# A depthwise convolution on four engines: four taps of the even places move to TensorE as float32 diagonal matmuls

## The chip, the cores and the metric

The kernel runs on one core of one Trainium2 chip. A core has TensorE (PE, with its weight loads shown as PEld), VectorE (DVE), ScalarE (ACT), GpSimd (POOL) and SyncE (SP, which issues most DMAs); each engine works through its own instructions in a fixed order and waits for others by semaphores. The metric is the device time of one execution in microseconds (us), lower is better.

## The reference

A decoder trunk with two layers on 1024 tokens of width 1024: a Conformer convolution layer, then a stick-breaking attention layer, each followed by a convolution-gated FFN with a per-layer embedding (PLE). Everything is float32. The part that matters here is the convolution module of the first layer, and the PLE product that needs nothing but the input p:

```python
def causal_dwconv(x, w, b):              # w: 31 taps x 1024 channels, one filter for each channel
    k = w.shape[0]
    y = lax.conv_general_dilated(
        x, w[:, None, :].astype(x.dtype), window_strides=(1,), padding=[(k - 1, 0)],
        dimension_numbers=("NWC", "WIO", "NWC"), feature_group_count=x.shape[-1])
    return y + b

def conformer_conv(x, pw1_w, pw1_b, dw_w, dw_b, ln_g, ln_b, pw2_w, pw2_b):
    h = x @ pw1_w + pw1_b                # 1024 -> 2048
    a, g = jnp.split(h, 2, axis=-1)
    h = a * jax.nn.sigmoid(g)
    h = causal_dwconv(h, dw_w, dw_b)
    h = layer_norm(h, ln_g, ln_b)
    h = jax.nn.silu(h)
    return h @ pw2_w + pw2_b
...
        ple = jax.nn.sigmoid(x @ ple_w_gate[i]) * (p[i] @ ple_w_proj[i])
```

## The kernel before

Products of matrices keep float32 accuracy by splitting each operand into a rounded high part and the rest (type float32r) and adding three matmuls (`mm3`, lines 136 to 139: high by high, high by low, low by high). Such a matmul with 512 columns is one instruction.

The stretch that the change touches is the first 311 us, phase 1 of the first layer. It goes over eight channel tiles c of 128 channels (`KT`, loop from line 528).

- **pw1(c)**, lines 466 to 481: for each half of 512 tokens, 48 matmuls into one of two PSUM tiles `big0` and `big1` (line 470); ACT takes the sigmoid of the gate part (`sg`, line 474), DVE multiplies and writes `hb` (line 476), even tokens in `hb[:, 0]`, odd tokens in `hb[:, 1]`.
- **depthwise(c)**, lines 483 to 522: the 31 taps by a fast two-phase scheme. With even and odd tokens apart, three filters are enough: even taps on even tokens (16 multiply-adds into PSUM `e`, lines 500 and 502), odd taps on odd tokens (15 into PSUM `o`, lines 507 and 509), and the summed taps on the sum of both (16 into `pb` in SBUF). DVE does the first two, one tap in an instruction of 128x512. The third is shared: ACT multiplies (`pr`, line 490), POOL adds (line 491). DVE then joins the three (lines 514, 516 and 520). `e` and `o` are PSUM banks 0 and 1.
- **weights**: for each channel tile two slabs come by DMA, ACT rounds them (line 132) and POOL makes the rest (line 86).
- **the fill**, `ple_proj` (lines 195 to 232): the PLE products of both layers, which depend on nothing before, in eight halves. A half transposes p twice (line 211, into PSUM), ACT and DVE split it into `pTh` and `pTl` (line 215 and line 86), then 24 matmuls for four output tiles, which ACT copies out (line 225) to DRAM. Transposes and products take PSUM banks 2 and 3 in turns (`sm_bank`).
- **after it**: `conv_ln` transposes the result of all channels back by tokens (line 545, into `big0` and `big1` in turns), takes the layer norm (DVE lines 169 to 180 and 547, ACT line 550), `conv_act` transposes again (line 559), takes SiLU (ACT line 562), rounds (line 565) and splits (DVE), and `pw2` multiplies (into PSUM banks). All this is done for the first 512 tokens, then for the others.

The order of the instructions on each engine isn't the order of the code: a scheduler with a model of the times lays out all of them when the kernel is built, by when it thinks that operands are ready. An engine then follows that order, whatever the real times are.

Of the kernel before, what the change touches and what calls it, by code (L numbers as in the profile page):

```python
# [8 lines left out]
F32 = mybir.dt.float32  # L9
# [4 lines left out]
ALU = mybir.AluOpType  # L14
PSUM = bass.MemoryType.PSUM
DRAM = bass.MemoryType.DRAM

P = 128
# [3 lines left out]
HALF = 512  # L22
# [9 lines left out]
NEG = -1.0e30  # L32
HP = 8
N_B = 16
AW = (5 + 6 + 7 + 8) * P
NA = 2
AHEAD = 1
# [14 lines left out]
def trunk_kernel(ctx: ExitStack, tc, x, p, a_pw1_w, a_pw1_b, a_dw_w, a_dw_b, a_ln_g, a_ln_b, a_pw2_w, a_pw2_b,  # L52
                 b_wq, kv_wk, kv_wv, b_wo, ln_mix_g, ln_mix_b, ffn_w_up, ffn_w_gate, ffn_conv_w, ffn_conv_b,
                 ffn_w_down, ple_w_gate, ple_w_proj, ln_ffn_g, ln_ffn_b, out, stop=None):
    nc = tc.nc
# [3 lines left out]
    def pool(name, bufs=1, stack=ctx, **kw):  # L59
        return stack.enter_context(tc.tile_pool(name=name, bufs=bufs, reuse_waits="tile", **kw))  # L60
# [10 lines left out]
    big0 = psum.tile([P, 1024], F32, name="big0")  # L71
    banks = [psum.tile([P, HALF], F32, name=f"bank{i}") for i in range(4)]

    def turns(tiles):
        tiles = list(tiles)

        def nxt():
            tiles.append(tiles.pop(0))
            return tiles[-1]

        return nxt

    bank, acc_bank, sm_bank = (turns(t) for t in (banks, banks[0:2], banks[2:4]))

    def sub_l(eng, l, full, h):
        eng.tensor_tensor(out=l, in0=full, in1=h.bitcast(F32), op=ALU.subtract)  # L86
# [7 lines left out]
    ident, vec_a, vec_b, zero = (ctile[:, a:b] for a, b in ((0, P), (P, 2 * P), (2 * P, 2 * P + 88), (350, 351)))  # L94
# [97 lines left out]
        nc.vector.scalar_tensor_tensor(out=dst, in0=dst, scalar=rstd, in1=b, op0=ALU.mult, op1=ALU.add)  # L192


    def ple_proj(i, sb, dst):

        pT, ws = [], []

# [211 lines left out]
    pp1 = dram.tile([S, D], F32, name="pp1")  # L410

    with ExitStack() as l0:
        big = turns((big0, pool("ps0", 1, l0, space=PSUM).tile([P, 1024], F32, name="big1")))
        res = []
        x1T = [None, None]
        with ExitStack() as ph:
# [5 lines left out]
            def pw1_w(c):  # L422
                return [load_w(w_slab(a_pw1_w[0], slice(0, KT), slice(o + c * P, o + (c + 1) * P)), (KT, P))
                        for o in (D, 0)]
# [54 lines left out]
                                                   op0=ALU.add, op1=ALU.mult)  # L479
                return hb  # L480

            def depthwise(c, hb):
                nc.vector.tensor_tensor(out=hb[:, 2, :], in0=hb[:, 0, :], in1=hb[:, 1, :], op=ALU.add)

                pb = sb.tile([P, HALF], F32, name="pb", bufs=2)
# [2 lines left out]
                for k in range(1, N_B):  # L488
                    pr = sb.tile([P, HALF], F32, name="pr", bufs=3)
                    nc.scalar.mul(pr, hb[:, 2, k:k + HALF], dws[:, c, k:k + 1])  # L490
                    nc.gpsimd.tensor_tensor(out=pb, in0=pb, in1=pr, op=ALU.add)  # L491
                e = acc_bank()
                o = acc_bank()
                os_ = sb.tile([P, 1 + HALF], F32, name="os", bufs=2)
                nc.gpsimd.memset(os_[:, 0:1], 0.0)
                ov = os_[:, 1:]
                for k in range(16):
                    v, w = hb[:, 0, k:k + HALF], dwc[:, c, 2 * k:2 * k + 1]
                    if k == 0:
                        nc.vector.tensor_scalar(out=e, in0=v, scalar1=w, scalar2=None, op0=ALU.mult)  # L500
                    else:
                        nc.vector.scalar_tensor_tensor(out=e, in0=v, scalar=w, in1=e, op0=ALU.mult, op1=ALU.add)  # L502
                    if k == 15:
                        break
                    v, w = hb[:, 1, k + 1:k + 1 + HALF], dwc[:, c, 2 * k + 1:2 * k + 2]
                    if k == 0:
                        nc.vector.tensor_scalar(out=o, in0=v, scalar1=w, scalar2=None, op0=ALU.mult)
                    else:
                        nc.vector.scalar_tensor_tensor(out=ov if k == 14 else o, in0=v, scalar=w, in1=o, op0=ALU.mult,  # L509
                                                       op1=ALU.add)  # L510
# [11 lines left out]

            ys = []
            rowp = Rows()
            fill = ple_proj(0, sb, pp0) + ple_proj(1, sb, pp1)
            w1 = pw1_w(1)
            hb = pw1(0, w0)
            for c in range(KT):
                w0, w1 = w1, pw1_w(c + 2) if c < KT - 2 else None
                nxt = pw1(c + 1, w0) if c < KT - 1 else None  # L530
                ys.append(depthwise(c, hb))
                hb = nxt
            for piece in fill:
                piece()
# [358 lines left out]
```

## Time and profile before

| | us |
|---|---|
| median of 3 runs (2700.6 to 2705.1) | 2701.26 |
| profiled execution, its own time | 2710.24 |
| its span, first to last instruction | 2708.1 |

| busy in the profiled execution | PE | DVE | ACT | POOL |
|---|---|---|---|---|
| whole span, us (share) | 2530.3 (93%) | 1797.4 (66%) | 1045.1 (39%) | 1219.6 (45%) |

Busy time of PE is modelled from overlapping instructions; for PE the distance from one start to the next is the better measure. A row of the timeline gives start, duration, engine, line of the code, output and input by name, count, and in brackets how long the engine had been idle and what it had waited for. A row of the groups by line gives the count, the sum and the mean duration (in ns), then the idle time before.

### The profile page before, as it was taken

Reading aid. Unit: us, or ns where it says so; the run is one execution under the profiler, and the core shown is the slowest. Engines: PE = TensorE matmul, PEld = TensorE weight load, DVE = VectorE, ACT = ScalarE, POOL = GpSimd, SP = SyncE. Lnnn points to the kernel's source line nnn. Section 1 sums busy time; section 2 is a strip of 40 time slices with the busy share of each in tenths; the row PEclk is TensorE's granted clock in tenths of the full one; section 3 lists DMA queues with packets and bytes.
Section 4 is the critical chain, followed back from the end, with each engine's and each line's share of the span. In section 5 each row is a group of like instructions: output and inputs, shape, how many; then the busy total and the mean of one; then the engine's idle time right before and its main releaser. Section 6 shows DMA issues by size and latency. Waiting matters only on the chain.

```text
span 2708.1 us, 34235 instructions
## 1 busy us (share of the span) xinstructions
PE 2530.3 (93%) x13300; PEld 2151.5 (79%) x13300; DVE 1797.4 (66%) x2785; ACT 1045.1 (39%) x1621; POOL 1219.6 (45%) x825
## 2 busy tenths in 40 slices
PE   8996898999999999999999999789899999999995
PEld 6884888987878787878888887589798787787874
DVE  4999769465565655675667677777845555655558
ACT  4556532333223332314555566632333232323231
POOL 3998236534333443413443433544744343333354
PEclk9998999999999999999999999899899999999998
DMA  4114421211111111123111101322111121111121
GB/s 151 47 47 148 163 71 63 86 47 50 47 60 47 55 55 55 40 80 108 46 43 36 55 25 47 129 84 87 63 63 62 48 63 47 47 47 47 47 78 62
DMA packets 149085, 179.12 MB, mean 66 GB/s; under 512 B 6508, under 2 KB 125756, under 8 KB 148924
## 3 DMA queue, kind: packets, MB, share of 16 engines
q1 hardware_dynamic: 144316, 168.56, 19.6%
q10 hardware_dynamic: 4608, 8.39, 0.8%
q8 instruction: 104, 1.70, 0.3%
q14 instruction: 57, 0.47, 0.1%
HBM read 151.76 MB, written 20.97 MB: 64 GB/s over the span
## 4 chain that ended last, share of the span: by engine, by line
PE 68%; DVE 18%; POOL 5%; DMA 3%; issue 3%; ACT 3%; SPq 0%; POOLq 0%; ACTq 0%; DVEq 0%
PE bank L137 13%; PE bank L138 13%; PE bank L139 13%; PE big L137 8%; PE big L139 7%; PE big L138 7%; POOL w L86 3%; PE big L739 2%; POOL pb L491 2%; DVE bank L502 2%; DVE bank L509 2%; DMA w<-in_ffn_w_up 2%; DVE pt L282 2%; PE bank L773 1%; PE more L779 1%
## 5 line engine op out<-in xcount | busy, mean ns | idle before, releaser
L86 POOL TENSOR_TENSOR w<-w 128x512 fp32r<-128x512 f32 (+1 forms) x444 | 757.7, 1720 | 1081.5 <-ACT w L299 697.0
L137 PE MATMUL bank<-w,xT 128*128 128x256 f32 x1280 | 369.7, 291 | 37.7 <-ACT sg L258 23.7
L299 ACT CAST w<-w 128x512 fp32r<-128x512 f32 x308 | 180.1, 619 | 540.2 <-PE bank L139 142.1
L138 PE MATMUL bank<-w,xT 128*128 128x256 f32 x1280 | 368.8, 290 | 2.1 <-POOL w L86 2.1
L139 PE MATMUL bank<-w,xT 128*128 128x256 f32 x1280 | 367.7, 290 | 0.7 <-DVE xT L86 0.6
L137 PEld LDWEIGHTS bank<-w,xT 128*128 128x128 f32 x1280 | 250.8, 197 | 41.0 <-ACT sg L258 25.1
L760 POOL TENSOR_TENSOR res<-res,rr 128x639 f32<-128x639 f32 (+3 forms) x96 | 152.6, 1590 | 259.7 <-DVE rr L758 237.9
L758 DVE TENSOR_TENSOR_SCAN rr<-rr,ctile 128x127 f32<-128x127 f32 (+7 forms) x128 | 195.7, 1550 | 102.5 <-ACT rr L756 102.1
L138 PEld LDWEIGHTS bank<-w,xT 128*128 128x128 f32 x1280 | 251.5, 197 | 3.4 <-POOL w L86 3.0
L139 PEld LDWEIGHTS bank<-w,xT 128*128 128x128 f32 x1280 | 250.2, 196 | 1.7 <-DVE xT L86 1.3
L132 ACT CAST w<-w 128x1024 fp32r<-128x1024 f32 x136 | 142.9, 1051 | 227.5 <-PE bank L138 60.5
L137 PE MATMUL big<-xT,w 128*128 128x512 f32 x544 | 212.3, 390 | 0.4 <-DVE xT L86 0.4
L138 PE MATMUL big<-xT,w 128*128 128x512 f32 x544 | 211.9, 389 | 0.0
L139 PE MATMUL big<-xT,w 128*128 128x512 f32 x544 | 211.9, 389 | 0.0
L294 DVE TENSOR_TENSOR w<-w 128x512 f32<-128x512 f32 x176 | 130.1, 759 | 106.1 <-DMA w<-in_ffn_w_up 52.1
L137 PE MATMUL bank<-xT,w 128*128 128x512 f32 x496 | 200.0, 403 | 0.3 <-DVE m L86 0.2
L138 PE MATMUL bank<-xT,w 128*128 128x512 f32 x496 | 198.2, 400 | 0.0
L139 PE MATMUL bank<-xT,w 128*128 128x512 f32 x496 | 197.8, 399 | 0.0
L383 DVE TENSOR_TENSOR m<-m,bank 128x512 f32<-128x512 f32 x192 | 128.8, 682 | 82.2 <-PE bank L139 82.1
L137 PE MATMUL bank<-w,f 128*128 128x512 f32 x448 | 170.3, 395 | 7.8 <-ACT f L366 4.3
L138 PE MATMUL bank<-w,f 128*128 128x512 f32 x448 | 176.1, 393 | 0.0
L139 PE MATMUL bank<-w,f 128*128 128x512 f32 x448 | 173.8, 391 | 0.0
(162 smaller groups left out, 5941.3 us busy)
## 6 DMA issues: line engine op xcount, KB each, us to landing
w<-in_ffn_w_gate SPq DMA_DIRECT2D x44, 512.0 KB
w<-in_ffn_w_up SPq DMA_DIRECT2D x44, 512.0 KB
w<-in_ffn_w_down SPq DMA_DIRECT2D x44, 512.0 KB
w<-in_a_pw_w SPq DMA_DIRECT2D x32, 512.0 KB
pp<-o ACTq DMA_DIRECT2D x32, 256.0 KB
w<-in_ple_w_gate SPq DMA_DIRECT2D x16, 512.0 KB
w<-pp SPq DMA_DIRECT2D x16, 512.0 KB
w<-in_b_wo SPq DMA_DIRECT2D x16, 512.0 KB
```

The lines of the kernel that those rows point to most:

```text
L86: eng.tensor_tensor(out=l, in0=full, in1=h.bitcast(F32), op=ALU.subtract)
L132: nc.scalar.copy(out=h[:, 0:n], in_=raw)
L137: nc.tensor.matmul(out=o, lhsT=sh, rhs=mh, start=first, stop=False)
L138: nc.tensor.matmul(out=o, lhsT=sh, rhs=ml, start=False, stop=False)
L139: nc.tensor.matmul(out=o, lhsT=sl, rhs=mh, start=False, stop=last)
L282: nc.vector.tensor_tensor(out=f, in0=a, in1=c, op=ALU.subtract)
L294: nc.vector.tensor_tensor(out=out, in0=a, in1=c, op=op)
L299: nc.scalar.copy(out=h, in_=full)
L383: nc.vector.tensor_tensor(out=rv, in0=rv, in1=ps, op=ALU.add)
L491: nc.gpsimd.tensor_tensor(out=pb, in0=pb, in1=pr, op=ALU.add)
L758: nc.vector.tensor_tensor_scan(out=rv[:, i, 1:n][:, ::-1], data0=rv[:, i, 1:n][:, ::-1], data1=zero.broadcast_to([P, n - 1]), initial=1.0, ...
L760: nc.gpsimd.tensor_tensor(out=av[:, :, 0:n - 1], in0=av[:, :, 0:n - 1], in1=rv[:, :, 1:n], op=ALU.mult)
```

## The change

For each channel tile the first four of the sixteen taps on the even tokens leave DVE. ACT writes four diagonal matrices of 128x128 (`dg`, identity times the tap's weight of each channel), and TensorE multiplies them with the shifted `hb`, four plain float32 matmuls of 512 columns that add up in the PSUM bank `e`. DVE adds the other twelve taps onto `e` as before. The matmuls stand in the code ahead of pw1(c+1).

PSUM is dealt out anew: `e` takes banks 0 and 1 in turns over the channel tiles, `o` is always bank 2, and the fill now takes bank 3 and the first halves of `big0` and `big1` in turns.

```diff
@@ -80,7 +81,7 @@
-    bank, acc_bank, sm_bank = (turns(t) for t in (banks, banks[0:2], banks[2:4]))
+    bank, acc_bank = (turns(t) for t in (banks, banks[0:2]))
@@ -410,7 +411,9 @@
-        big = turns((big0, pool("ps0", 1, l0, space=PSUM).tile([P, 1024], F32, name="big1")))
+        big1 = pool("ps0", 1, l0, space=PSUM).tile([P, 1024], F32, name="big1")
+        big = turns((big0, big1))
+        sm_bank = turns((banks[3], big0[:, 0:HALF], big1[:, 0:HALF]))
@@ -479,7 +482,17 @@
-            def depthwise(c, hb):
+            def first_taps(c, hb):
+
+                e = acc_bank()
+                dg = sb.tile([P, N_PE, P], F32, name="dg", bufs=2)
+                for k in range(N_PE):
+                    nc.scalar.mul(dg[:, k], ident, dwc[:, c, 2 * k:2 * k + 1])
+                for k in range(N_PE):
+                    nc.tensor.matmul(out=e, lhsT=dg[:, k], rhs=hb[:, 0, k:k + HALF], start=(k == 0), stop=(k == N_PE - 1))
+                return e
+
+            def depthwise(c, hb, e):
@@ -489,16 +502,13 @@
-                e = acc_bank()
-                o = acc_bank()
+                o = banks[2]
...
-                    if k == 0:
-                        nc.vector.tensor_scalar(out=e, in0=v, scalar1=w, scalar2=None, op0=ALU.mult)
-                    else:
+                    if k >= N_PE:
                         nc.vector.scalar_tensor_tensor(out=e, in0=v, scalar=w, in1=e, op0=ALU.mult, op1=ALU.add)
@@ -522,13 +532,14 @@
             for c in range(KT):
                 w0, w1 = w1, pw1_w(c + 2) if c < KT - 2 else None
+                e = first_taps(c, hb)
                 nxt = pw1(c + 1, w0) if c < KT - 1 else None
-                ys.append(depthwise(c, hb))
+                ys.append(depthwise(c, hb, e))
                 hb = nxt
```

The scheduler lays out the first 320 us anew; from the first columns of pw2 on, the instructions stand on all engines as before. A line of the new code stands 1 to 11 below the same line of the old (line 211 is now 212, line 137 is 138, line 545 is 556, line 559 is 570); the new matmul is line 492.

On PE at the end of pw1(7): `big` and `bank` are PSUM, `praw` the input p, `pTh` and `pTl` its halves. Before, the fill follows, and what is ready of the first token tiles is transposed at once (line 545, five channel tiles of eight):

```order
L139 MATMUL big_100<-xT,w 128x512
L211 MATMUL bank_85<-ctile,praw 128x128 x4
L137 MATMUL bank_84<-w,pTh 128x512
L138 MATMUL bank_84<-w,pTh 128x512
L139 MATMUL bank_84<-w,pTl 128x512
...
L545 MATMUL big_81<-ctile,res 128x128 x5
```

Now, the four taps of the last channel tile (line 492) stand between the fill's first instructions:

```order
L140 MATMUL big_100<-xT,w 128x512
L212 MATMUL big_81<-ctile,praw 128x128 x4
L138 MATMUL bank_85<-w,pTh 128x512
L139 MATMUL bank_85<-w,pTh 128x512
L492 MATMUL bank_83<-hb,dg 128x512 x4
L212 MATMUL big_100<-ctile,praw 128x128 x4
L140 MATMUL bank_85<-w,pTl 128x512
```

For each of the seven channel tiles before, the four stand after the first 27 matmuls of the next tile's pw1. No transposes of line 545 stand near here any more.

On PE around the layer norm: before, the last transposes of line 545 for the first four token tiles stand among the last two halves of the fill, and those of line 559 too (the last half's):

```order
L211 MATMUL bank_84<-ctile,praw 128x128 x4
...
L211 MATMUL bank_85<-ctile,praw 128x128 x4
L559 MATMUL bank_82<-ctile,m 128x128
L559 MATMUL bank_83<-ctile,m 128x128
L545 MATMUL big_81<-ctile,res 128x128 x8
L559 MATMUL bank_82<-ctile,m 128x128
L559 MATMUL bank_83<-ctile,m 128x128
L545 MATMUL big_100<-ctile,res 128x128 x8
L137 MATMUL bank_84<-w,pTh 128x512
```

Now, the first transposes of line 556 (the old 545) stand ahead of the last 12 matmuls of the whole fill, and all others behind them:

```order
L212 MATMUL big_100<-ctile,praw 128x128 x4
L556 MATMUL big_81<-ctile,res 128x128 x8
L138 MATMUL bank_85<-w,pTh 128x512
L139 MATMUL bank_85<-w,pTh 128x512
L138 MATMUL big_100<-w,pTh 128x512
...
L140 MATMUL bank_85<-w,pTl 128x512
L556 MATMUL big_100<-ctile,res 128x128 x8
L556 MATMUL big_81<-ctile,res 128x128 x8
L570 MATMUL bank_82<-ctile,m 128x128
L570 MATMUL bank_83<-ctile,m 128x128
L556 MATMUL big_100<-ctile,res 128x128 x8
```

The layer norm of the first four token tiles has moved from among the fill to its end.

## Rows read from the trace of the kernel before

**Rows 1.** Busy time by stretch: length, engines (instructions), granted clock, DMA share, GB/s
```profile
28.90:204.10 175.20, 175.20 (x770) 144.95 (x771) 153.24 (x213) 91.25 (x126) 147.76 (x109) 0.99 0.17 51
204.10:275.10 71.00, 49.18 (x197) 35.82 (x195) 69.03 (x99) 46.58 (x75) 58.37 (x43) 0.88 0.45 152
275.10:311.30 36.20, 31.16 (x194) 26.47 (x193) 24.10 (x98) 26.84 (x39) 4.75 (x2) 0.95 0.36 126
```
**Rows 2.** Chain that ended last, from 28.9 to 311.3, shares by line
```profile
by line: POOL pb L491 17.1%; DVE bank L502 16.4%; DVE bank L509 15.5%; issue 4.8%; DVE hb L476 4.5%; DVE hb L483 3.6%; POOL w L86 2.9%; PE big L137 2.2%; DVE pb L516 2.1%; PE big L138 2.0%; PE big L139 1.9%; PE bank L137 1.9%; DMA pp<-o 1.7
```
**Rows 3.** Timeline of PE in pw1: start, duration
```profile
49.57 0.39 PE L137 MATMUL big<-xT,w 128*128 128x512 f32 x1
49.80 0.39 PE L138 MATMUL big<-xT,w 128*128 128x512 f32 x1
...
203.71 0.40 PE L139 MATMUL big<-xT,w 128*128 128x512 f32 x1
```
**Rows 4.** Groups by line, 28.9 to 275.1: busy us, mean ns
```profile
L491 POOL TENSOR_TENSOR pb<-pb,pr 128x512 f32<-128x512 f32 x120 | 158.0, 1323 | 9.0 <-ACT pr L490 2.8
...
L86 POOL TENSOR_TENSOR w<-w 128x1024 fp32r<-128x1024 f32 x20 | 48.9, 2446 | 30.8 <-ACT w L132 30.8
...
L476 DVE SCALAR_TENSOR_TENSOR hb<-big,ctile,sg 128x512 f32<-128x512 f32 x16 | 18.4, 1148 | 20.1 <-ACT sg L474 20.1
L483 DVE TENSOR_TENSOR hb<-hb 128x527 f32<-128x527 f32 x8 | 14.8, 1854 | 0.0
```
**Rows 5.** Timeline of DVE: two taps, the last `hb`, the last join
```profile
205.79 0.76 DVE L502 SCALAR_TENSOR_TENSOR bank<-hb,taps,bank 128x512 f32<-128x512 f32 x1
206.45 0.76 DVE L509 SCALAR_TENSOR_TENSOR bank<-hb,taps,bank 128x512 f32<-128x512 f32 x1
...
213.03 1.13 DVE L476 SCALAR_TENSOR_TENSOR hb<-big,ctile,sg 128x512 f32<-128x512 f32 x1
...
274.45 0.68 DVE L520 TENSOR_TENSOR res<-pb,bank 128x512 f32<-128x512 f32 x1
```
**Rows 6.** Timeline of PE over one half of the fill
```profile
267.56 0.60 PE L211 MATMUL bank<-ctile,praw 128*128 128x128 f32 x4
268.40 0.65 PE L211 MATMUL bank<-ctile,praw 128*128 128x128 f32 x4 [0.24 <-ACT o L225]
270.31 0.50 PE L137 MATMUL bank<-w,pTh 128*128 128x512 f32 x1 [1.26 <-DVE pTl L86]
...
272.35 0.50 PE L137 MATMUL bank<-w,pTh 128*128 128x512 f32 x1 [0.39 <-DVE pTl L86]
...
276.87 0.60 PE L211 MATMUL bank<-ctile,praw 128*128 128x128 f32 x4
```
**Rows 7.** Timeline of PE: transposes of plain float32
```profile
4.74 1.94 PE L152 MATMUL big<-ctile,res 128*128 128x128 f32 x8 [4.74 <-DMA res<-in_x]
...
285.88 1.03 PE L545 MATMUL big<-ctile,res 128*128 128x128 f32 x8
286.75 0.38 PE L559 MATMUL bank<-ctile,m 128*128 128x128 f32 x2
```
**Rows 8.** Timeline of DVE: layer norm of the first two token tiles
```profile
276.96 2.49 DVE L169 BATCH_NORM_STATS2 norm<-big 128x6 f32<-128x512 f32 x4 [1.83 <-PE big L545]
...
282.61 0.28 DVE L547 SCALAR_TENSOR_TENSOR norm<-norm 128x1 f32<-128x1 f32 x2
```
**Rows 9.** Timeline of ACT in layer norm and SiLU of the first 512 tokens
```profile
295.82 1.28 ACT L562 ACT_TABLE_LOAD   x1
297.11 1.45 ACT L562 ACTIVATE pt<-bank,ctile 128x512 f32<-128x512 f32 x2
...
310.18 1.15 ACT L565 CAST xT<-pt 128x512 fp32r<-128x512 f32 x2
```
**Rows 10.** Groups by line of ACT, whole span: small operations, and the norm
```profile
L727 ACT CAST m<-bank 128x128 fp32r<-128x128 f32 x64 | 17.0, 272 | 32.1 <-DVE m L86 23.4 <-PE bank L139 8.2
...
L550 ACT ACTIVATE m<-big,norm 128x1024 f32<-128x1024 f32 x8 | 9.4, 1207 | 4.8 <-DVE norm L547 4.4 <-ACT o L225 0.4
```

More of the change, by code (lines that the diff above doesn't have):

```diff
@@ L34 @@
 N_B = 16
+N_PE = 4
 AW = (5 + 6 + 7 + 8) * P
@@ L192, in layer_norm, with ple_proj @@
         nc.vector.scalar_tensor_tensor(out=dst, in0=dst, scalar=rstd, in1=b, op0=ALU.mult, op1=ALU.add)
-    def ple_proj(i, sb, dst):
+    def ple_proj(i, sb, dst, sm_bank):
         pT, ws = [], []
@@ L524, in trunk_kernel @@
             rowp = Rows()
-            fill = ple_proj(0, sb, pp0) + ple_proj(1, sb, pp1)
+            fill = ple_proj(0, sb, pp0, sm_bank) + ple_proj(1, sb, pp1, sm_bank)
             w1 = pw1_w(1)
```

## The prediction

> **What bounds the kernel now.** I read the busy time by stretch first, then the chain of waits, then the timelines of the engines it names.
>
> The stretch that the change touches falls into three parts [rows 1]. From 28.9 to 204.1 us PE is busy without a gap with the 768 matmuls of pw1, while DVE (153 of 175 us) and POOL (148) are nearly full too. From 204.1 to 275.1 DVE is the full one (69 of 71 us), since it is behind with the taps; PE does the fill, with gaps, and the granted clock falls to 0.88 in the mean. From 275.1 to 311.3 comes the layer norm with the rest of the fill beside it. The chain that ended last runs in the main through DVE and POOL here: 16.4% and 15.5% at the two tap lines, 17.1% at POOL's adds, and some 2% at each line of PE's pw1 [rows 2]. By the chain alone, taps taken from DVE are a gain. But a chain names one path, and the work goes to an engine with no gap in the longest part.
>
> In pw1 one matmul of 512 columns starts each 0.228 us (49.57 to 49.80, and the last at 203.71) [rows 3], so a channel tile costs PE 96 x 0.228 = 21.9 us. A tap on DVE starts each 0.66 us [rows 5]: 31 x 0.66 = 20.5, with two `hb` writes of 1.15, the sum of 1.85 and three joins of about 0.7 [rows 4, 5] some 26.7 us. POOL has 15 adds of 1.32 and two weight subtractions of 2.45: 24.7 us [rows 4].
>
> **What the change removes.** 32 instructions of 0.66 us on DVE, 21 us in all, 2.6 for a channel tile: 26.7 becomes 24.1. POOL keeps its 24.7.
>
> **What it adds.** ACT writes 32 diagonals; the nearest row is a cast of 128x128 at 0.27 us [rows 10], so 1.1 us for a channel tile. ACT is busy 91 of 175 us [rows 1] and has its diagonals a channel tile ahead, so I cost it at nothing; without that cover it would be 1.1 us for a tile, 9 in all.
>
> PE gets 32 float32 matmuls of 512 columns that are no transposes, which the trace doesn't show. From below, a float32r one of that size takes 0.228 us [rows 3]. From above, the slowest float32 row is the transpose of 128 columns at the start, 1.94/8 = 0.24, four times that 0.97; the later ones take 0.87/8 = 0.109 (285.88 to 286.75), four times that 0.44 [rows 7]. I take 0.91, four float32r matmuls: this kernel needs three for high and low parts and leaves low by low out, and the full product has all four; 0.97 is the end it is nearest to. So four taps cost PE 3.65 us for a channel tile, 21.9 becomes 25.5, and PE is now the slowest of the three.
>
> The Trainium skill, page "FP8 and Floating Point Precision", section "TensorE Precision Notes", says that a true float32 product makes four passes through the array, high and low of each operand against each other. By it a tap is an estimated 0.91 us as well and the sum the same; no run here shows it yet.
>
> **The sum**, from the last matmul of pw1 to the last rounding of SiLU for the first 512 tokens, which ends at 310.18 + 1.15 = 311.33 before [rows 9]. The point behind it is the same work in the same order.
>
> 1. pw1 ends at 203.94. Seven groups of four taps stand ahead of that end: 28 x 0.91 = 25.5, so 229.4. The start of pw1 I leave where it is. PE is not held up by the others: at 25.5 us for a tile DVE (24.1) and POOL (24.7) keep pace, and a tap's `hb` is due 27 matmuls, 6.2 us, after pw1 of its tile.
> 2. Depthwise ends earlier: some 24.7 us behind the last `hb`, at about 258 in place of 275.1 [rows 5]. That is the gain, and it is worth nothing unless PE is free for the layer norm then.
> 3. PE isn't. In its order the first transposes of the layer norm stand ahead of the last 12 matmuls of the fill, all others behind them. Before, the fill started at 204 and had 71 us beside DVE's backlog, and its last third covered the layer norm's latency. Now it starts at 229.4.
> 4. The first half of the fill holds the last four taps: about 3 us for the sigmoid and `hb`, 3.65 for the taps, 5.5 for the matmuls and transposes left: 241.6.
> 5. Six more halves. One took 9.3 us from 267.56 to 276.87, with 1.89 us of waits and a little of the norm between [rows 6]: without these it is 7.2. Three PSUM buffers in place of two take away the wait for copies between halves, not the one for rounding and subtracting p. I take 8.5: 51, so 292.6.
> 6. Half of the last one up to the norm's transposes: 5.5, so 298.1.
> 7. From there to the last rounding. A token tile takes 0.9 for transposes [rows 7], about 3 for statistics and small operations on DVE (two took 5.9, with work for the fill between) [rows 8] and 1.2 for ACT [rows 10]. Only two `big` tiles are there, so the third waits for the first and the fourth for the second, whose transposes stand behind the 12 fill matmuls: the fourth is out of ACT after about 15.3. Then the table load of 1.28 and eight SiLUs of 0.66 and roundings of 0.53, with two norms of the next tokens between them, 12 to 13 [rows 9, 10]. Together 29.3, so 327.4.
>
> 327.4 - 311.3 = 16 us later. Behind that point PE is the bound again and nothing on another engine was late, so the 16 us go to the end: 2710.2 + 16 = 2726 for the profiled execution. That one was 9 us above the median of the runs; against the median it is 2701.3 + 16 = **2717**.
>
> Its own range: a tap at 0.97 adds 1.9, at 0.68 (three passes) it takes 7.4; a half of the fill between 7.2 and 9.3 is -8.6 to +5.3 over 6.6 halves; the tail between 24 (ACT and one tile's latency alone) and 33 is -5 to +4. They don't all go one way: 2706 to 2730. The float32r end of a tap, 0.228, would take 28 x 0.68 = 19 us.
>
> **Rivals.**
>
> - *DVE's relief comes through, faster.* If a float32 tap is about as cheap as the float32r row, PE ends pw1 6.4 us later in place of 25.5, and if the third buffer takes half the waits out of the fill (7.6 for a half) and the tail is 26, the sum is 16 - 19 - 6 - 3 = -12: 2689. It decides at a tap below some 0.4 us. For it: the chain of waits stands on DVE and POOL [rows 2], and PE idles 22 of 71 us after pw1 [rows 1]. Against it: float32 transposes, which only move data, already cost 0.109 us for 128 columns, where the float32r matmul costs 0.057. 9%.
> - *No change.* The taps cost what I say, but the gaps of PE after pw1 take them up: halves of 7.2 us without a wait and a tail of 24 make 16 - 8.6 - 5.3 = 2 us: 2703. Or the taps cost half, 0.456: 16 - 12.7 = 3 us, 2705. For it: 22 us of gaps and the slow clock of that part [rows 1]; against it: the wait for `pTl` [rows 6] is a chain through three engines that the change leaves alone. 16%, 5 of it for half the price. The footnote on peak rates in the Trainium skill's "Perfetto Trace Analysis", section "Engine Utilization", halves the array's rate for a kind of float32, which stands behind that half price; no row here bears it out.
> - *A new wait, slower still.* PE works in order, so a tap that waits for `hb` holds the next pw1 back. Before, DVE wrote the last `hb` at 213.03, 9 us after pw1's end, and was that late only because it fell behind by 2 us or so in each tile [rows 3, 5]. If DVE or POOL still falls behind, from 6.2 us on the tap waits: some 4 us in each of five tiles, 20 us, so 2737. Against it: 24.1 and 24.7 are below 25.5. 8%.
>
> **How the numbers follow.** The forecast has 67%. The time is 2717. Leaving out most of the faster rival and half of the slow one, the range is 2700 to 2732. A measurement of this kernel can tell about 0.2%, 5.4 us, from no change: faster by more than that 0.09, within it 0.16, slower 0.75.
>
> **What would show it.** The new matmuls at about 0.9 us from start to start; pw1's matmuls at 0.228 with no gap, the last at about 229; DVE's last join near 258, with gaps on DVE in every channel tile; the fill on PE up to about 300; the last rounding of SiLU near 327; every stage behind it shifted by one amount. I am wrong in the size if the taps start below 0.8 us apart, and in the reason if PE has gaps between a tap and the next pw1, if the fill's halves take 7.5 us or less, or if a later stage takes up the delay.

## The result: slower, by twice what was forecast

| | before | changed |
|---|---|---|
| median of the runs | 2701.5 us (4 runs) | 2742.4 us (4 runs, 2732.9 to 2744.1) |
| ratio, 95% interval | | 1.0133 [1.0112, 1.0154] |
| profiled execution, its span | 2710.2, 2708.1 us | 2743.0, 2741.2 us |

The ratio is the one on record; the two medians divide to 1.015, because the kernel before came out at 2701.5 here and at 2704.5 to 2706.9 in four later sets of 9 to 24 runs, beside which 2742.4 is 1.013 to 1.014. On a second occasion the changed kernel had 2744.0 us, ratio 1.0138 [1.0120, 1.0155]. The forecast was 2717 us, 2700 to 2732: the direction was right, the size was not.

The changed kernel's busy time by stretch: first projection, from its end to the first product of the second projection, and from there to the first transposes of a normalised token tile (length, PE, PEld, DVE, ACT, POOL, granted clock, DMA share, GB/s):

```profile
31.10:230.60 199.50, 199.49 (x834) 155.82 (x835) 171.11 (x227) 108.35 (x171) 166.52 (x126) 1.00 0.14 41
230.60:329.10 98.50, 73.35 (x330) 54.41 (x327) 57.01 (x122) 50.54 (x79) 40.62 (x27) 0.91 0.47 158
329.10:388.80 59.70, 52.73 (x426) 51.88 (x424) 41.64 (x112) 19.68 (x25) 16.56 (x7) 0.94 0.35 124
```

The second and third of these in the kernel before (its first is in [rows 1]):

```profile
204.10:303.00 98.90, 72.14 (x321) 54.42 (x319) 87.28 (x186) 65.12 (x102) 60.72 (x44) 0.90 0.42 145
303.00:355.80 52.80, 50.86 (x422) 50.09 (x420) 41.84 (x94) 18.79 (x24) 18.10 (x8) 1.00 0.49 167
```

DVE is busy 30 us less in the second stretch, and the stretch is as long as before. With the start of pw1, the 33 us of the spans come apart into four terms:

| term | forecast | measured |
|---|---|---|
| start of pw1 | 0 | 31.1 - 28.9 = +2.2 |
| pw1 | 28 x 0.91 = +25.5 | 199.5 - 175.2 = +24.3 |
| end of pw1 to pw2 (for the forecast: to the last SiLU rounding) | -9.4 | 98.5 - 98.9 = -0.4 |
| pw2 | 0 | 59.7 - 52.8 = +6.9 |
| sum | 16 | 33.0 |

The third row has two ends, since the forecast's last point, the last SiLU rounding for the first 512 tokens, lies some us behind pw2's first product. Measured to that point (338.99 now, 311.33 before) the stretch is 108.4 us in place of 107.4, +1.0 where -9.4 was forecast; the other 5.5 us of the 33 then lie behind it. From the end of pw2 both spans run alike to the end. The taps in pw1, PE's timeline (start, duration), which answers to [rows 3]:

```profile
85.04 0.39 PE L140 MATMUL big<-xT,w 128*128 128x512 f32 x1
85.27 3.60 PE L492 MATMUL bank<-hb,dg 128*128 128x512 f32 x8
88.30 0.79 PE L138 MATMUL big<-xT,w 128*128 128x512 f32 x1
```

Four taps take 88.30 - 85.27 = 3.03 us, 0.76 each; the trace has two records for each of them. There is no gap on PE in pw1 (busy 199.49 of 199.50 us). The last group is another case (PE, then DVE beside it):

```profile
230.23 0.39 PE L140 MATMUL big<-xT,w 128*128 128x512 f32 x1
...
237.20 6.07 PE L492 MATMUL bank<-hb,dg 128*128 128x512 f32 x8 [4.59 <-DVE hb L479]
243.11 0.60 PE L212 MATMUL big<-ctile,praw 128*128 128x128 f32 x4
```

```profile
231.44 3.92 DVE L512 SCALAR_TENSOR_TENSOR bank<-hb,taps,bank 128x512 f32<-128x512 f32 x5
235.39 0.75 DVE L524 SCALAR_TENSOR_TENSOR res<-bank,ctile,os 128x512 f32<-128x512 f32 x1
236.06 1.09 DVE L479 SCALAR_TENSOR_TENSOR hb<-big,ctile,sg 128x512 f32<-128x512 f32 x1
...
266.40 0.69 DVE L530 TENSOR_TENSOR res<-pb,bank 128x512 f32<-128x512 f32 x1
```

DVE works in order and wrote the last `hb` behind five taps and a join, though the sigmoid was there at 231.35 (230.66 + 0.69 on ACT); PE waited 4.59 us, and the taps then took 5.9 us, at a granted clock of 0.60 from 237.2 to 243.2. The last join of the depthwise stage ended at 267.09 (before: 275.13 [rows 5]). The first of the rows below, the layer norm's first transposes, starts 40 us later, on PE, behind the fill; the last rounding of SiLU on ACT answers to [rows 9]:

```profile
306.79 1.09 PE L556 MATMUL big<-ctile,res 128*128 128x128 f32 x8 [0.24 <-ACT o L226]
...
316.23 1.97 PE L556 MATMUL big<-ctile,res 128*128 128x128 f32 x8 [4.67 <-ACT m L561]
...
324.42 0.69 PE L570 MATMUL bank<-ctile,m 128*128 128x128 f32 x2 [3.72 <-ACT m L561]
...
351.58 0.58 PE L138 MATMUL bank<-w,xT 128*128 128x256 f32 x1 [6.35 <-DVE m L598]
```

```profile
338.36 0.63 ACT L576 CAST xT<-pt 128x512 fp32r<-128x512 f32 x1
```

In the kernel before, fill products stood between these waits, and the first two token tiles' transposes were partly done during the fill. The wait of 6.35 us in the last row of PE is most of the 6.9 us of pw2. The chain that ended last, by line from 31.1 to 339.0, beside [rows 2]: PE now holds what DVE and POOL held.

```profile
by line: PE big L138 20.7%; PE big L139 20.4%; PE big L140 20.4%; PE bank L492 7.8%; POOL pb L504 3.4%; PE bank L138 3.1%; PE bank L140 2.8%; PE bank L139 2.4%; issue 1.9%; ACT o L226 1.8%; ACT pTh L216 1.5%; DVE bank L519 1.5%; PE big L556
```

### The profile page after: what moved, and what is told of

Read it like the earlier page. It is cut to its first block, busy times and chain, and to the rows that moved or that the text cites. A ratio compares the mean times of both kernels' runs of the same rounds, so it can differ in the third digit from the quotient of the medians.

```text
span 2741.2 us, 34371 instructions
## 1 busy us (share of the span) xinstructions
PE 2558.0 (93%) x13364; PEld 2165.8 (79%) x13364; DVE 1783.0 (65%) x2753; ACT 1051.0 (38%) x1653; POOL 1220.0 (45%) x825
## 4 chain that ended last, share of the span: by engine, by line
PE 76%; DVE 13%; POOL 3%; DMA 3%; ACT 2%; issue 2%; SPq 0%; ACTq 0%; DVEq 0%; POOLq 0%
PE bank L138 13%; PE bank L139 13%; PE bank L140 13%; PE big L138 10%; PE big L140 9%; PE big L139 9%; POOL w L87 2%; PE big L750 2%; DMA w<-in_ffn_w_up 2%; DVE pt L283 1%; PE bank L784 1%; PE more L790 1%; PE more L789 1%; DVE w L295 1%; DVE tT L87 1%
## 5 line engine op out<-in xcount | busy, mean ns | idle before, releaser
L138 PEld LDWEIGHTS bank<-w,xT 128*128 128x128 f32 x1280 | 253.2, 199 | 45.1 <-ACT sg L259 24.3
```

What stands on the lines that cost most here:

```text
L138: nc.tensor.matmul(out=o, lhsT=sh, rhs=mh, start=first, stop=False)
```

## The experiments

Two theories stood at the start: A, the longer list of PE is all of the 33 us; B, about half is the new dealing of PSUM banks, which puts the whole fill ahead of the layer norm. The table has each kernel's median, its ratio to the kernel before with the interval, and from its profiled execution the same boundaries as above: start of pw1, length of pw1, from its end to pw2, pw2, and the time at which the first feed-forward stage has its first product on transformed inputs (FFN). What comes behind FFN takes between 2125 and 2148 us on PE in these executions, and the matmuls there are as many in all of them; it tells nothing of the change (see the last section). Because of it a total and its FFN can differ by 10 us and more, and FFN is the better of the two for what the change does. Two executions of the changed kernel differ by 7 us at FFN, so a single boundary is good to some us.

| kernel | median us | ratio | start | pw1 | to pw2 | pw2 | FFN |
|---|---|---|---|---|---|---|---|
| before | 2701.5 to 2706.9 | 1 | 28.9 | 175.2 | 98.9 | 52.7 | 534.7 |
| changed | 2742.4 | 1.0133 [1.0112, 1.0154] | 31.1 | 199.5 | 98.5 | 59.7 | 567.7 |
| e16 changed again | 2744.0 | 1.0138 [1.0120, 1.0155] | 32.1 | 201.5 | 99.7 | 64.5 | 574.6 |
| e1 no tap on PE | 2715.0 | 1.0041 [1.0026, 1.0056] | 31.1 | 177.5 | 105.4 | 60.0 | 553.7 |
| e12 two taps | 2722.6 | 1.0065 [1.0050, 1.0080] | 31.6 | 189.8 | 100.0 | 62.8 | 562.1 |
| e11 eight taps | 2770.3 | 1.0233 [1.0218, 1.0248] | 35.1 | 222.6 | 102.0 | 60.0 | 596.7 |
| e3 four taps, twice | 2769.8 | 1.0234 [1.0216, 1.0252] | 31.6 | 224.0 | 101.4 | 59.7 | 596.2 |
| e2 one pass | 2725.2 | 1.0081 [1.0062, 1.0100] | 31.5 | 182.0 | 105.1 | 65.4 | 559.7 |
| e4 `o` in SBUF | 2787.4 | 1.0301 [1.0283, 1.0319] | 34.4 | 246.0 | 85.8 | 72.5 | 618.0 |
| e5 late fill on small banks | 2732.1 | 1.0098 [1.0085, 1.0111] | 33.7 | 198.6 | 95.7 | 51.8 | 559.0 |
| e10 the same, and columns | 2728.5 | 1.0076 [1.0061, 1.0092] | 30.6 | 199.9 | 95.0 | 50.9 | 552.7 |
| e6 loads from GpSimd | 2738.8 | 1.0121 [1.0107, 1.0136] | 31.0 | 199.5 | 99.8 | 60.0 | 567.8 |
| e9 early residuals | 2727.0 | 1.0074 [1.0061, 1.0086] | 35.9 | 202.0 | 107.8 | 52.6 | 575.1 |
| e7 last tile on DVE | 2744.2 | 1.0150 [1.0129, 1.0171] | 31.5 | 200.7 | 103.4 | 60.0 | 571.8 |
| e13 changed, half the fill | 2700.8 | 0.9974 [0.9961, 0.9987] | 30.6 | 201.5 | 65.8 | 60.0 | 534.7 |
| e14 before, half the fill | 2695.4 | 0.9959 [0.9944, 0.9975] | 30.4 | 174.7 | 89.7 | 59.9 | 532.5 |
| e8 e1 with e5 | 2705.0 | 0.9998 [0.9987, 1.0009] | 30.6 | 175.3 | 95.4 | 53.4 | 529.7 |
| e15 e1 with e10 | 2700.1 | 0.9977 [0.9966, 0.9989] | 30.9 | 174.4 | 91.3 | 52.0 | 528.1 |

### The price of the matmuls: e1, e12, e11, e3, e2

e1 puts the taps back on VectorE and keeps the new banks:

```diff
-                e = first_taps(c, hb)
+                e = acc_bank()
...
-                    if k >= N_PE:
+                    if k == 0:
+                        nc.vector.tensor_scalar(out=e, in0=v, scalar1=w, scalar2=None, op0=ALU.mult)
+                    else:
```

> The changed kernel with its first four taps back on VectorE; only the new dealing of PSUM banks is kept (e in turn in two banks, o in a third, the small tiles on one bank and on halves of the two big tiles). Two theories for the 33 us between the spans (2708.1 and 2741.2), of which 16 were forecast. Theory A, the matmuls: all of it is TensorE's longer list, 32 tap matmuls of 0.76 us (24.3 us), the wait and the slow clock of the last four (7.5 us); then this kernel, which has none of them, is at the time of the kernel before, 2700 to 2706 us. Theory B, the dealing: about half is not the matmuls but what the new banks do to the order after them. The layer norm's transposes need the big tiles, which the fill now holds, so all of the fill stands ahead of them on TensorE, where before some 30 of its products stood between them; and the eight residual loads stand behind a blocked weight load on SyncE, which leaves TensorE waiting 6.35 us in the second projection. Both are also in this kernel's order, so by B it is at 2713 to 2722 us, with the wait at the second projection of 5 to 7 us to be seen.

2715.0 us: theory B's range, and the wait at pw2 is there (6.87 us). A alone falls. The size is less sure than the total says: FFN comes 19.0 us later than in the kernel before, and what stands behind it took 17.6 us less in this execution.

e3 has `for k in list(range(N_PE)) * 2` around the matmuls, e11 `N_PE = 8`, e12 `N_PE = 2`:

> Every group of four tap matmuls is issued twice (the second start overwrites the first, so nothing of the result changes). If each us on TensorE in the first projection goes to the end, 28 x 0.76 = 21.3 us are added there and 3 to 6 for the last group: 24 to 27 us over the changed kernel, 2766 to 2770 us. The rival that part of the taps runs where TensorE would have waited anyway has it at less than 15 us over, under 2757 us.

> Eight taps as matmuls in place of four, dealing as in the changed kernel. TensorE has as many matmuls as in the third experiment (each four twice, 2769.8 us), VectorE four taps less for a channel tile (21 us less in all). If VectorE's relief is worth nothing, since TensorE is the last one, the time is that of the third experiment within 4 us: 2766 to 2774 us. If the relief shortens the stretch behind the first projection, where VectorE was the full engine before the change, the time is 5 to 12 us lower: 2758 to 2765 us.

> Two taps as matmuls, dealing as in the changed kernel. With none it is 2715 us (the first experiment), with four 2742, with four twice 2770: 6.8 us for a tap, 0.85 for each of the eight matmuls that it stands for, against 0.76 in the trace. If the cost is in proportion, two cost 13 to 14 us over the first experiment: 2727 to 2731 us. If VectorE's relief were worth something for the first few taps, as long as it is the last one, the time lies under the line: 2715 to 2723 us.

e3 came out at 2769.8 us and e11 at 2770.3, both as expected: VectorE's four further taps less bring nothing. In pw1's length the price is in proportion: 12.3, 22.0 and 46.5 us (e12, changed, e3) over e1 for 14, 28 and 56 matmuls ahead of its end, 0.88, 0.79 and 0.83 us for each; e11 has 45.1, 0.81 for each. e12's total, 2722.6 us, lies under the line, in the rival's range. Where that comes from is the stretch behind pw1: 105.4 us in e1, 100.0 in e12, 98.5 in the changed kernel. In this dealing the first two taps do give 5 us back there. But e1 also waits for loads of p in that stretch (3.75 and 2.82 us, the longest), and with the dealing mended (e8 without taps on PE, e5 with four, below) it is 95.4 and 95.7 us: no relief.

e2 stores `hb` and the diagonals rounded (`F32R` in place of `F32` in both tiles):

> The tap matmuls on rounded operands in one pass (hb and the diagonal matrices are stored rounded, which leaves out the low parts of these values), all else as in the changed kernel. The trace of the changed kernel has 3.03 us for four of them (0.76 each) against 0.228 us for a rounded 128x512 product: 28 of them in the first projection stage get shorter by 0.53 us each, 14.9 us, and the last four by 2 or more. Theory A and theory B agree that TensorE's list sets the pace while the first projection runs, so both have it 14 to 19 us under the changed kernel: 2723 to 2729 us. The rival that VectorE and GpSimd, at 24.1 and 24.7 us for a channel tile against TensorE's 25.2, were already as late has it gain less than 5 us: 2737 or more, with the end of the depthwise stage where it was (267 us).

2725.2 us, in the range expected, but in part by luck. pw1 is 17.5 us shorter than in the changed kernel, as it should be (14.9 expected); the way to pw2 and pw2 are 12.3 us longer, FFN comes only 8.0 us earlier, and the rest of the gain lies behind FFN. Four taps take 0.93 us now (84.27 - 83.34):

```profile
83.34 1.10 PE L492 MATMUL bank<-hb,dg 128*128 128x512 f32 x4
84.27 0.39 PE L139 MATMUL big<-xT,w 128*128 128x512 f32 x1
```

### The dealing of banks: e4, e5, e10, e8, e15

```diff
-        sm_bank = turns((banks[3], big0[:, 0:HALF], big1[:, 0:HALF]))
+        sm_bank = turns(banks[2:4])
...
-                o = banks[2]
+                o = sb.tile([P, HALF], F32, name="oo", bufs=1)
```

> The taps stay matmuls; the fill has its two small banks of the kernel before again and leaves the big tiles alone, and the odd accumulator o is moved from its bank to SBUF to make room. In this order the layer norm's transposes stand between the fill's products again, and the residual loads ahead of the weights that block. Theory A (the matmuls): at most 2 us of change, 2740 to 2744 us, since TensorE's list is as long as before. Theory B (the dealing): 10 to 17 us of the 33 come back, 2725 to 2732 us; the wait of 6.35 us at the second projection is gone and the fill's last products stand in the layer norm's waits. What could spoil it: VectorE's taps of o from SBUF instead of PSUM, if they take other than 0.66 us.

2787.4 us, far from both: the last sentence's case came. Groups by line (busy us, mean ns):

```profile
L519 DVE SCALAR_TENSOR_TENSOR oo<-hb,taps,oo 128x512 f32<-128x512 f32 x104 | 140.3, 1349 | 1.5
```

A tap of `o` takes 1.35 us in the mean from SBUF to SBUF, against the 0.76 of a tap with PSUM [rows 5], POOL's adds take 1.57 us against 1.32 [rows 4], and pw1, waiting for `hb`, grows to 246.0 us (why, see the last section). Part of the fill now stands behind pw2's first product, which makes the way to pw2 short and pw2 long in the table. It says nothing on the dealing. e5 does it without that:

```diff
-ple_proj(1, sb, pp1, sm_bank)
+ple_proj(1, sb, pp1, turns((banks[3], banks[0])))
```

> As the changed kernel, taps as matmuls, but the second half of the fill (pieces 21 to 40) turns over two small banks, the fourth and the first (the first is free once the seventh channel tile is joined), and leaves the big tiles to the layer norm. In this kernel's order the layer norm's transposes stand from the fifth half of the fill on between its products, and six of the eight residual loads stand ahead of the weight load that blocks SyncE. Theory B (the dealing of banks): the 4.67 and 3.72 us that TensorE waits in the layer norm and the 6.35 at the second projection are filled or gone, so 10 to 18 us come back: 2724 to 2732 us; first product of the second projection near 317 us instead of 329. Theory A (the longer list alone): 2738 to 2744 us.

2732.1 us, at the upper end of B's range; pw2's first product came at 328.0, not at 317: the start was 2.6 us later and the fill, now with the layer norm in it, ended at 319.7. pw2 is back at 51.8 us. e10 adds a `col_bank = turns(banks[2:4])` for the small vectors:

> The fifth experiment (second half of the fill on two small banks) with one more piece of the old dealing: the transposes of the small vectors at the start turn over the two small banks again, not over halves of the big tiles. If these big halves made the start of the first projection late (33.7 us in the fifth experiment, 31.1 in the changed kernel, 28.9 before), it starts within 1 us of 29 and the time is 2 to 5 us below the fifth experiment: 2727 to 2730 us. Then what is left against the kernel before, 23 to 26 us, is the matmuls' own 24.3. The rival is that the start is set by the order of the loads alone: no gain, 2731 to 2733.

2728.5 us is in the range; the start, 30.6 us, is not within 1 us of 29, so only a part of the late start is from these banks. What is left at FFN, 18.0 us, is less than its 1.7 at the start and 24.7 more in pw1, since this kernel gains 3.9 us between pw1 and pw2, 1.8 in pw2 and 2.7 from there to FFN. e8 is e1's and e5's edit together, e15 e1's and e10's:

> All taps on VectorE, as in the first experiment, with the banks of the fill's second half as in the fifth: the layer norm's transposes stand between the fill's products again and the residual loads ahead of all but three weights. Theory B: the 8 us (4 to 12) by which the first experiment was slower than the kernel before are gone, 2699 to 2707 us, no difference from before. If instead something else of the new dealing cost them (the later start, 31.1 in place of 28.9 us, or three banks for the accumulators), it stays at 2711 to 2716 us.

> All taps on VectorE, the new banks for the accumulators, the fill's second half on two small banks as in the eighth experiment, and the small vectors at the start on the two small banks as in the tenth: the parts of the dealing that cost nothing or gained. In the eighth experiment the profiled execution reached the first feed-forward stage 5 us earlier than the kernel before; an earlier start of the first projection (30.6 there, 28.9 before) would add 1 to 2. 2696 to 2703 us beside a kernel before at 2702 to 2706; the rival is that the later stages' own scatter hides it, no difference.

Both as expected: 2705.0 us, no difference from before, and 2700.1, 0.23% under it (0.11 to 0.34%). e15 is the version that beats both kernels, with no tap on PE. At FFN, e5 against e8 (29 us, 3 of them a later start) and e10 against e15 (25 us) give the matmuls alone, with the dealing equal. In pw1's length these pairs have 23.3 and 25.5 us, 0.83 and 0.91 for each of 28 matmuls.

### pw2: e6, e9

pw2 adds its product to the layer's input x, scaled; eight loads (`m<-in_x`) bring x, called the residual. SyncE's queue in the changed kernel, and DVE behind it:

```profile
314.75 30.76 SPq L131 DMA_DIRECT2D w<-in_a_pw_w  x2
345.56 4.28 SPq L584 DMA_DIRECT2D m<-in_x  x8
```

```profile
349.77 1.23 DVE L585 SCALAR_TENSOR_TENSOR m<-m 128x1024 f32<-128x1024 f32 x1 [2.40 <-DMA m<-in_x]
```

The second of the two weight loads waited 30.1 us on SyncE, until a product of pw2 itself had ended (line 140, 344.95) and its place was free. Before, the first four residual loads were issued at 309.82. e6 has `nc.gpsimd.dma_start` for them:

> As the changed kernel, but the eight residual loads of the second projection are issued by GpSimd, so they don't stand behind the weight load on which SyncE is blocked from 314.75 to 345.56 us. If the wait of 6.35 us at the second projection comes from this order on SyncE, it goes and the time is 5 to 7 us lower, 2735 to 2738 us. The rival is that the loads would land no earlier or that TensorE then waits for weights at the same place: 2741 to 2744 us.

2738.8 us is in neither range, and the wait is still 6.37 us: on GpSimd the loads stood behind a weight's subtraction and were issued at 345.26. The edit did not do what it was for. e9 issues four of them ahead of the layer norm:

```diff
+            early = []
+            for t in range(4):
+                early.append(slot())
+                nc.sync.dma_start(out=early[t], in_=x2d[t * P:(t + 1) * P, :])
...
-                    r = slot()
-                    nc.sync.dma_start(out=r, in_=x2d[t * P:(t + 1) * P, :])
+                    r = early[t] if half == 0 else slot()
+                    if half == 1:
+                        nc.sync.dma_start(out=r, in_=x2d[t * P:(t + 1) * P, :])
```

> As the changed kernel, but the four residual loads of the second projection's first half are issued before the layer norm, ahead of the two weight loads in SyncE's order (on GpSimd, in the sixth experiment, they still stood behind a weight's subtraction and were issued at 345.3 us, as late as before). If VectorE's wait for them (2.40 and 0.68 us) and its backlog behind them make the 6.35 us that TensorE waits at the second projection, that wait shrinks to 3 us or less and the time falls by 3 to 6 us: 2736 to 2740 us. The rival is that VectorE's statistics of the seventh and eighth token tile, which stand ahead of the first scaling of a residual until 347.4 us, make the wait: then it stays above 5 us and the time at 2741 to 2744.

```profile
362.16 0.39 PE L138 MATMUL bank<-w,xT 128*128 128x256 f32 x1 [0.66 <-DVE m L604]
```

The wait is 0.66 us and pw2 takes 52.6 us as before the change, so the late loads are its 6.9 us. The other runs agree: where the residual loads stand behind that blocked weight load (e1, e2, e3, e7, e11, e12, e13, e16), PE waits 6.5 to 8.5 us there, and where the first of them are issued ahead of it (before, e5, e8, e10, e15), pw2 takes 51 to 53 us. Even e14 below has the wait, with the banks and taps of the kernel before:

```profile
317.05 0.58 PE L137 MATMUL bank<-w,xT 128*128 128x256 f32 x1 [6.50 <-DVE m L587]
```

That the 6.9 us also come back at the end, e9 doesn't show: its start, pw1 and its way to pw2 are 4.8, 2.5 and 9.3 us longer, and FFN came 7 us later than in the changed kernel. The total, 2727.0, missed low for another reason: the stages behind FFN took 23 us less (last section).

### From pw1 to pw2: e7, e13, e14

e7 calls `first_taps` only for `c < KT - 1`:

> As the changed kernel, but the first four taps of the last channel tile are on VectorE again; seven groups of matmuls stay. It takes from TensorE the 4.59 us for which the last group waits for hb, and its 5.9 us at the low clock, 10.5 us in all, if these are a cost of their own: 2730 to 2734 us. The rival is that TensorE waits at that place anyway, for the first rounded pieces of p, and that VectorE's four more taps (2.6 us) end the depthwise stage later without cost: then only the matmuls' own 3 to 5 us are gained, 2736 to 2740 us.

2744.2 us: no gain, both ranges missed. PE now waits at the same place for ACT:

```profile
238.18 0.80 PE L138 MATMUL bank<-w,pTh 128*128 128x512 f32 x1 [5.56 <-ACT pTh L216]
```

and the loads of p, which waited 6.5 us (3 times) for transposes in the changed kernel, waited longer. SyncE's own waits, 200 to 350 us, e7 (total us, times, longest):

```profile
SPq L208 <- DMA praw<-in_p: 30.8, 12, 3.4
SPq L208 <- PE big L212: 25.3, 13, 4.4
```

So the last group's 10.5 us can't be taken out by itself: the fill's own chain fills the place. e13 and e14 halve the fill, in the changed kernel and in the kernel before. They leave out the PLE product of the second layer, whose feed-forward stage reads the first layer's instead, so they give another result:

```diff
-            fill = ple_proj(0, sb, pp0, sm_bank) + ple_proj(1, sb, pp1, sm_bank)
+            fill = ple_proj(0, sb, pp0, sm_bank)
...
-        ffn_phase(1, x3T, res, pp1,
+        ffn_phase(1, x3T, res, pp0,
```

> The changed kernel with only half of the fill: the projection of p for the second feed-forward stage is left out, and that stage reads the first one's product (another result). From the end of the first projection to the first product of the second one it is 98.5 us in the changed kernel and 98.9 in the kernel before, although the depthwise stage ends 36 us behind the first projection in the one and 70 in the other. Theory: the fill is what takes the relief of VectorE, because it is as long and stands on TensorE ahead of the layer norm. Then four halves less (8.7 us each) bring the layer norm forward: 45 us for the fill and the last taps, 22 behind it, 67 us for the stretch, and the time falls by about 31 us to 2706 to 2716 us. The rival is that the layer norm's own chain through VectorE and ScalarE sets the stretch: less than 12 us, 2731 or more.

> The same with the kernel before: half of the fill left out, all taps on VectorE. By the theory its stretch is held by VectorE's taps, whose last join comes 70 us behind the first projection, with some 24 us of layer norm behind that: 94 us in place of 98.9, so 3 to 7 us less and at most 7 back at the second projection, where the residual loads now stand behind a weight load that blocks: 2696 to 2708 us. The changed kernel's 33 us then shrink to about 10 when the fill is halved in both. By the rival (the fill doesn't matter for the relief) both lose the same.

The stretch from pw1 to pw2, e13, then e14:

```profile
232.00:297.90 65.90, 46.20 (x202) 35.04 (x200) 51.78 (x111) 35.88 (x54) 36.00 (x25) 0.84 0.36 124
```

```profile
205.10:294.80 89.70, 47.93 (x189) 36.87 (x187) 79.26 (x159) 49.74 (x75) 58.31 (x43) 0.70 0.26 88
```

65.9 us (67 expected) and 89.7 (94). Half of the fill is worth 33 us to the changed kernel and 9 to the kernel before, and the two differ by 5 us in place of 38. In the second DVE is busy for 79 of 90 us, in the first for 52 of 66. The totals, 2700.8 and 2695.4 us, are 5 and 1 under the ranges; the stages behind FFN took 17 and 16 us less than in the profile of before. These two differ in their banks as well as in their taps; no run halves the fill with the dealing equal.

> The changed kernel once more, beside the others on one chip: 2733 to 2744 us, 1.011 to 1.015 of the kernel before; its profiled execution reaches the first product of the first feed-forward stage 33 us (30 to 35) later than the kernel before, and what its total lies under or over that comes from the feed-forward stages, where TensorE waits 2.9 or 1.0 us at the down projection.

2744.0 us, at the upper edge; FFN came 39.9 us after that of the kernel before, not 30 to 35: the stretches of one kernel vary by 1 to 5 us between executions, pw2 most.

## Why the prediction missed by half

*Step 1, the end of pw1: right in sum, partly by luck.* 229.4 was forecast, 230.6 came. A tap starts each 0.76 us, not 0.91. In pw1's length it costs, with what stands around a group, 0.79 to 0.91 us, by the kernels that are compared; against e1, which has this dealing, 0.79. The rest is the start, left where it was, that came 2.2 us later, and 2.3 us that pw1 has longer in e1 too. No gap on PE in pw1: "PE is not held up by the others" held. By the Trainium skill's "FP8 and Floating Point Precision", section "TensorE Precision Notes", true float32 takes four passes, an estimated 0.91 us here; the trace doesn't agree, it has 3.3 times the float32r product, and two records for each matmul. The half price after the footnote in the Trainium skill's "Perfetto Trace Analysis", section "Engine Utilization", 0.456, is not borne out.

*Step 2, the depthwise stage: right in direction.* It ends at 267 in place of 275, not at 258: the last `hb` was done at 237.15, 6.5 us behind pw1, and from there DVE took 29.9 us in place of 24.7. It didn't matter: PE was not free, as step 3 said.

*Steps 4 to 7, the step that failed: -9.4 forecast, +1.0 measured to the same point.* The first half of the fill ended at 249.16 in place of 241.6, and 6.3 of the 10.4 us were lost here: the last taps started 6.6 us behind pw1 where I had 3, because DVE's order puts five taps and a join ahead of the last `hb`, and they took 5.9 us in place of 3.65, at a granted clock of 0.60. The next six and a half halves took 57.6 us to 306.8 (56.5 forecast), the tail 32.2 (29.3). But the forecast's larger error is to expect the stretch to shrink at all: e7 takes the last taps away, and something else waits in their place. With the taps on PE the stretch is set by the fill's chain (load of p, transposes, rounding on ACT, subtraction on DVE, products) and then the layer norm's, one after the other. Before, the fill ran beside DVE's 70 us of taps and part of the layer norm ran among the fill. e13 and e14 show that the fill is what takes the relief (half a fill is worth 33 us with the taps on PE, 9 us without), and e11 against e3 that more relief of DVE brings nothing. The dealing of banks is worth only 3 us here and 8 in pw2 (e5, e10).

*"Behind that point ... nothing on another engine was late": false.* Eight residual loads were, behind a weight load that waits for pw2's own first products. The forecast took a common order behind that point for common times, and did not ask what the second of the two weight loads ahead of them waits for. In pw2 it cost 6.9 us, and e9 shows it.

*The base.* Of the 25 us between 2717 and 2742, some 17 are these steps. The other 8: I took 9 us off because the profile of before lay that much over the median of three runs. The later sets put that kernel's median at 2704.5 to 2706.9, so its profile lay only 3 to 6 us over it, and three runs were too few for this step. The changed kernel's profile lies at its median.

*The rivals.* "DVE's relief comes through" fell by the tap's price and by e11 against e3, "no change" by the result and the way from pw1 to pw2. "A new wait" named the right wait in the wrong place: once, at the last channel tile, because DVE's order put `hb` behind taps, not in five tiles by falling behind; e7 shows that without it something else waits there.

## What to carry to other kernels

In this kernel work moved from a backlogged engine to one without a gap cost its full price, and the relief was worth nothing, because what the first engine held up stood behind other work on the second one as well. Ask what else stands on the receiving engine between there and the next stage, and halve that in an experiment. A change of buffers that comes with a change of work is a change of its own, which the scheduler answers with another order of every queue: run it alone. For each load that is moved behind another transfer, ask what that transfer waits for.

## What was not expected of the hardware

*A wait and the clock in the feed-forward stage.* Executions of one kernel differ by up to 18 us here (before: 2695.3 to 2713.2 in 24 runs). A part of it is seen at the down projection, where PE waits for DVE four times in each feed-forward stage. Of the eight waits one is short (1.7 us, the others 2.85) in the changed kernel's first profile, which took 2148.0 us behind FFN on PE, and three are (1.5 to 1.7) in its second, which took 2143.5. In e9 all eight are (0.96 to 1.5), and it took 2124.7. The changed kernel, and two windows from the end of the wait on; then e9:

```profile
814.25 0.50 PE L138 MATMUL big<-w,f 128*128 128x512 f32 x1 [2.85 <-DVE m L384]
```

```profile
814.20:816.20 2.00, 1.95 (x7) 1.55 (x8) 2.00 (x4) 0.81 (x2) 0.00 (x0) 0.81 0.00 0
816.20:818.20 2.00, 2.00 (x7) 1.52 (x6) 1.82 (x3) 0.55 (x2) 0.00 (x0) 0.50 0.00 0
```

```profile
815.92 0.50 PE L138 MATMUL big<-w,f 128*128 128x512 f32 x1 [0.96 <-DVE m L384]
```

```profile
815.90:817.90 2.00, 1.98 (x9) 1.65 (x10) 2.00 (x4) 0.82 (x2) 0.00 (x0) 1.00 0.00 0
817.90:819.90 2.00, 2.00 (x10) 1.65 (x9) 1.79 (x3) 0.55 (x2) 0.00 (x0) 1.00 0.00 0
```

After the wait of 2.85 us the granted clock falls to 0.50, the lower of the two levels, for some 2 us; after 0.96 it stays at 1.00. From the first product of the down projection in that stage to attention's first scores it is 612.5 us in e9, with four short waits, and 625.3 in the changed kernel with four long ones. The four compute engines have the same order in this stage in both kernels, so it is a matter of times; what decides between the two was not tried.

*Operands in SBUF.* In e4 a VectorE tap with both operands and the output in SBUF took 1.35 us in the mean, one with an accumulator in PSUM 0.75 as ever. It isn't SBUF alone, as GpSimd beside it shows:

```profile
310.30 1.62 POOL L504 TENSOR_TENSOR pb<-pb,pr 128x512 f32<-128x512 f32 x1
311.95 0.74 DVE L519 SCALAR_TENSOR_TENSOR oo<-hb,taps,oo 128x512 f32<-128x512 f32 x1
312.61 0.74 DVE L512 SCALAR_TENSOR_TENSOR bank<-hb,taps,bank 128x512 f32<-128x512 f32 x1
...
313.38 3.49 POOL L504 TENSOR_TENSOR pb<-pb,pr 128x512 f32<-128x512 f32 x2 [1.46 <-ACT pr L503]
...
314.59 1.13 DVE L519 SCALAR_TENSOR_TENSOR oo<-hb,taps,oo 128x512 f32<-128x512 f32 x1
```

Of the 104 taps of `oo`, seven ran while GpSimd ran nothing, and took 0.74 to 0.75 us each. The twelve that ran wholly within its operations took 1.1 to 2.9. A tap with its accumulator in PSUM took 0.74 to 0.76 in both cases.
